# The instruction order of a hybrid attention block, made with another machine model of the scheduler

## The chip, the cores and the metric

The kernel runs on one core of one Trainium2 chip. The metric is the device time of one execution in microseconds (us). The core has five instruction streams, each worked off in its own order: PE (matmuls and transposes), DVE and POOL (elementwise work), ACT (activations and copies), and SP, which here only issues DMAs. An instruction waits for others by semaphores.

## The reference, cut to what matters

One encoder block, sequence 1024, width 1024, all in float32:

```python
h_in = rms_norm(x, norm_mix_g, 1e-6)
qa, ka, va, qb, kb, vb, ga, gb = split(h_in @ w_in)         # 512 512 512 512 512 512 1024 1024
qa, ka, qb, kb = apply_rope(...)                             # pairs of 32 in heads of 64
ya = dilated_window_attention(qa, ka, va) @ w_branch_a       # 8 heads, windows 128/512/2048 at dilation 1/4/16
o  = (softmax(q1 k1^T / 8) - lam * softmax(q2 k2^T / 8)) @ v # 4 heads: differential attention
yb = (rms_norm(o, subln_g, 1e-5) * (1 - lam_init)) @ w_branch_b
x  = x + (sigmoid(ga) * ya + sigmoid(gb) * yb) @ w_out
h2 = rms_norm(x, norm_mlp_g, 1e-6)
x  = x + square(relu(h2 @ w_ff1)) @ w_ff2                    # 1024 -> 4096 -> 1024
return rms_norm(x, norm_final_g, 1e-6)
```

## The kernel before

**Arithmetic.** Every product of float32 operands is three matmuls: each operand is split into a high part in a reduced format and a low part (`hi` by a copy on ACT, L245, and `lo` by a subtraction on POOL or DVE, L246), and hi·hi, hi·lo and lo·hi are added in PSUM. The large projections also use one level of a Strassen-like scheme with seven products for eight (`first_products`, L254; `rest_operands`, L262; `rest_products`, L274): DVE forms sums and differences of weight blocks (L265 to L268), then two groups of 24 matmuls (banks `y…` and `z…`) and one of 12 (`4…`), and DVE moves the banks out with additions (L288, L289 for `y`; L292, L294, L295 for `z`; L298 for `4`). The next group that takes the same bank has to wait for these.

**Stages.** Up to about 140 us: the first norm, the transposes and the value projections. 140 to 435 us: eight pairs of column blocks of q and k (`qk_pair`, named q8, q12, q10, q14, q0, q4, q2, q6 in this order) take turns with eight pairs of gate columns (`gate_rest`, named g4 to g7, then g0 to g3). Each finished q or k tile is rotated (`rope`, L488): four small DMAs copy the tile with its blocks of 32 rows swapped (L493, tile `rot`), DVE multiplies by the sine (L494), POOL by the cosine (L495), DVE adds (L496), ACT and DVE split into hi and lo (L504, L505), and ACT stores both. 435 to 640 us: the differential attention, four heads of eight query blocks (`b_scores`, `b_combine`, `b_values`); for each block two score banks on PE (`sb`, L689), a minimum on DVE (L692), an exponential on ACT (L694), transposes back (`tb`), a split of the result (L614 on ACT, L615 on DVE), products with v. Between them stand the remaining two products of every gate (`gate_first`, L617: banks `g1_n` and `g2_n`, 12 matmuls each, moved out by L628 on ACT). 640 to 866 us: the dilated windows; then the merge and w_out, the first MLP product to 1322, the second to 1617, and the last rows of the second MLP product with the final norm.

**What sets the order.** The source is Python that issues operations in one order. A scheduler in the framework then makes the order of each engine: it runs the program on a model of the machine, in the model's own time, and puts next on each engine the instruction that is ready there, the earlier one of the source first. So the same source gives another order when the model gives operations other durations. Semaphore waits and the turns of buffers follow from the order. The choice of the model is an argument of `tile.TileContext` (L1466), with the default in the kernel before.

## Time and profile before

| | us |
|---|---|
| three runs | 1664.23, 1668.82, 1673.82 (median 1668.82) |
| the profiled execution | 1674.86 |
| its span | 1673.1 |
| mean granted PE clock in it | 0.972 of full speed |

The profile is of one execution. A busy time is the sum over an engine's instructions, a wait is idle time of an engine in front of an instruction, put down to what released it. In rows of the timeline the first number is the start in us from the span's start, the second the length.

### The profile page before, as it was taken

The numbers are of one execution on the slowest core, as the hardware profiler recorded it, in microseconds if no ns is written. First come the engines' busy times: TensorE is split into PE (matmuls) and PEld (weight loads), VectorE is DVE, ScalarE is ACT, GpSimd is POOL, SyncE is SP. The second block draws the span as 40 slices with busy tenths as digits, with TensorE's granted clock in tenths as the row PEclk, the third lists the DMA queues.
The fourth block names the chain that finished last, engine by engine and source line by source line (L and its number), as shares of the span: only waits on it lengthen the run. The fifth ranks groups of instructions, "written<-read, shape, count | busy, mean of one in ns | idle before, by whom it ended". The sixth has DMA issues, their size and how long they took to land. (4 is left out here: it accounts for less than half of the span.)

```text
span 1673.1 us, 20932 instructions
## 1 busy us (share of the span) xinstructions
PE 1557.9 (93%) x7832; PEld 1299.2 (78%) x7832; DVE 1181.4 (71%) x1367; ACT 697.6 (42%) x1064; POOL 585.3 (35%) x289
## 2 busy tenths in 40 slices
PE   8899889988789998989999999899999989999998
PEld 6798667766577887988887878687888867888776
DVE  5976798698688996645547357644355599898984
ACT  4432122232467774544433236444444552333331
POOL 1534444555232332012220003533333344354551
PEclk8999899998999999999999999999999999999999
DMA  6367566555767557656557333444333571423112
GB/s 214 125 210 215 164 196 223 175 184 163 263 194 233 200 191 271 204 180 215 156 162 278 110 130 94 120 128 130 114 101 101 179 268 51 163 74 116 51 38 101
DMA packets 214389, 271.23 MB, mean 162 GB/s; under 512 B 12784, under 2 KB 136848, under 8 KB 214288
## 3 DMA queue, kind: packets, MB, share of 16 engines
q1 hardware_dynamic: 200464, 236.33, 44.4%
q10 hardware_dynamic: 13824, 33.56, 5.3%
q8 instruction: 62, 1.02, 0.3%
q14 instruction: 39, 0.32, 0.1%
HBM read 183.81 MB, written 80.27 MB: 158 GB/s over the span
## 5 line engine op out<-in xcount | busy, mean ns | idle before, releaser
L1359 PE MATMUL p<-b,a 128*128 128x512 f32 x392 | 154.7, 395 | 5.1 <-DVE b L1274 5.1
L1358 PE MATMUL p<-b,a 128*128 128x512 f32 x392 | 154.2, 393 | 3.0 <-ACT a L1273 3.0
L1360 PE MATMUL p<-b,a 128*128 128x512 f32 x392 | 154.4, 396 | 2.0 <-DVE a L1274 1.9
L1274 POOL TENSOR_TENSOR b<-ws,b 128x1024 fp32r<-128x1024 f32 x20 | 61.4, 3088 | 95.3 <-ACT b L1273 85.3
L1359 PEld LDWEIGHTS p<-b,a 128*128 128x128 f32 x392 | 74.2, 189 | 23.0 <-DVE b L1274 6.0
L1274 POOL TENSOR_TENSOR b<-rb,b 128x1024 fp32r<-128x1024 f32 x21 | 70.8, 3390 | 54.7 <-ACT b L1273 46.7
L1360 PEld LDWEIGHTS p<-b,a 128*128 128x128 f32 x392 | 74.0, 189 | 20.1 <-DVE a L1274 3.9
L1358 PEld LDWEIGHTS p<-b,a 128*128 128x128 f32 x392 | 74.1, 189 | 19.8 <-ACT a L1273 3.4
L689 PE MATMUL sb<-kb,qb 128*128 128x512 f32 x256 | 74.7, 416 | 15.1 <-ACT p L694 8.8
L694 ACT ACTIVATE p<-sb,mn 128x1024 f32<-128x1024 f32 x64 | 71.3, 1116 | 38.5 <-DVE mn L692 23.7
L692 DVE TENSOR_REDUCE mn<-sb 128x1 f32<-128x1024 f32 x64 | 76.8, 1217 | 9.7 <-PE sb L689 9.2
L265 DVE TENSOR_TENSOR s<-w 128x512 f32<-128x512 f32 x15 | 16.2, 1081 | 85.8 <-DMA w<-in_w_ff 85.8
L156 POOL TENSOR_SCALAR n_y<-n_ss 128x1 f32<-128x1 f32 x23 | 5.1, 222 | 187.7 <-ACT n_xn L163 183.2
L803 PE MATMUL sa<-kh_a,zq 128*128 128x256 f32 x256 | 68.9, 300 | 1.2 <-DVE mna L812 1.2
L828 DVE TENSOR_TENSOR pta<-ta,pta 128x512 fp32r<-128x512 f32 x64 | 43.8, 688 | 33.9 <-ACT pta L827 33.7
L689 PEld LDWEIGHTS sb<-kb,qb 128*128 128x128 f32 x256 | 45.9, 192 | 27.9 <-ACT p L694 13.1
L1273 ACT ACTIVATE a<-fs 128x1024 fp32r<-128x1024 f32 x28 | 29.4, 1054 | 90.6 <-PE p L1359 71.3
L803 PE MATMUL sa<-kl_a,zq 128*128 128x256 f32 x256 | 65.8, 288 | 0.0
L246 POOL TENSOR_TENSOR wt_f_l<-w,wt_f_h 128x1024 fp32r<-128x1024 f32 x15 | 36.1, 2404 | 83.0 <-ACT wt_f_h L245 70.2
L816 ACT ACTIVATE sm<-sm,mna 128x512 f32<-128x512 f32 x64 | 46.1, 720 | 32.4 <-DVE mna L812 31.8
L827 ACT ACTIVATE pta<-ta 128x512 fp32r<-128x512 f32 x64 | 37.6, 591 | 52.2 <-PE ta L823 44.5
L1145 ACT ACTIVATE c<-c 128x512 f32<-128x512 f32 x64 | 39.9, 624 | 46.6 <-DVE c L292 34.9
(442 smaller groups left out, 4966.4 us busy)
## 6 DMA issues: line engine op xcount, KB each, us to landing
w<-in_w_in SPq DMA_DIRECT2D x32, 512.0 KB, 4.3
qk<-r ACTq DMA_DIRECT2D x32, 512.0 KB, 4.8
f<-c ACTq DMA_DIRECT2D x64, 256.0 KB, 2.0
rb<-in_w_ff SPq DMA_DIRECT2D x32, 512.0 KB, 4.6
ra<-f SPq DMA_DIRECT2D x64, 256.0 KB, 5.0
w<-in_w_ff SPq DMA_DIRECT2D x30, 512.0 KB, 4.2
vb<-vb SPq DMA_DIRECT2D x16, 512.0 KB, 6.6
rot<-raw SPq DMA_DIRECT2D x64, 128.0 KB, 4.5
```

The source lines that it names most:

```text
L689: nc.tensor.matmul(sps[:, 512 * n:512 * n + 512], q[:, z, (qb % 4) * P:(qb % 4 + 1) * P], o.k[m][:, 512 * n:512 * n + 512], start=z == 0, ...
L692: nc.vector.tensor_reduce(mn, sps, axis=AX.X, op=ALU.min)
L694: nc.scalar.activation(p, sps, AF.Exp, scale=-1.0, bias=mn, accum_out=o.zz[qb][:, m:m + 1])
L803: nc.tensor.matmul(ps[:, 0:CM], zq[:, n % 4, c, :], kk[:, c * CM:(c + 1) * CM], start=c == 0 and kk is o.kh, stop=c == NCLS - 1 and kk is ...
L816: nc.scalar.activation(sm, sm, AF.Exp, scale=-1.0, bias=mn, accum_out=stat[h % 2][:, n:n + 1])
L827: nc.scalar.activation(view[0], tv, AF.Copy)
L828: nc.vector.tensor_tensor(view[1], tv, f(view[0]), op=ALU.subtract)
L1145: nc.scalar.activation(c, c, AF.Relu)
L1274: eng.tensor_tensor(lo, x, f(hi), op=ALU.subtract)
L1358: nc.tensor.matmul(acc, ah[:, i % 2, c], bh[:, i % 2, :], start=i == 0 and not more, stop=False, skip_group_check=bool(more))
L1359: nc.tensor.matmul(acc, ah[:, i % 2, c], bl[:, i % 2, :], start=False, stop=False, skip_group_check=bool(more))
L1360: nc.tensor.matmul(acc, al[:, i % 2, c], bh[:, i % 2, :], start=False, stop=last, skip_group_check=bool(more))
```

## The change

The scheduler's order is made on its timeline machine in place of its default, the core simulator. The operations of the source stay. Every engine has as many instructions as before, apart from semaphore instructions; their order is other.

```diff
-    with tile.TileContext(nc) as tc:
+    with tile.TileContext(nc, schedule_with_timeline_sim=True) as tc:
         tile_hybrid_block(tc, t, out)
```

What that moves is seen at three places. Numbers behind names are those of the program's tiles.

DVE in the projections, before, from behind the last eviction of pair q14 (`raw15`, at 266.2 us): sums of the weights of g0 and q0 (`w1_90`, `w1_80`), the evictions of gate g7 (`gc70`, `gc71`), and the rope of tile 14.

```order
L265 TENSOR_TENSOR s1_g0_2529<-w1_91_2351 128x512
L266 TENSOR_TENSOR w1_91_2351<-w1_90_2349,w1_91_2351 128x512
L289 TENSOR_TENSOR gc70_2257<-yg7_2277,gu7_2256 128x512
L267 TENSOR_TENSOR w1_80_2252<-s1_q0_2417,w1_80_2252 128x512
L267 TENSOR_TENSOR w1_90_2349<-s1_g0_2529,w1_90_2349 128x512
L268 TENSOR_TENSOR w1_80_2252<-w1_80_2252 128x512
L268 TENSOR_TENSOR w1_90_2349<-w1_90_2349 128x512
L494 SCALAR_TENSOR_TENSOR rot14_2353<-rot14_2353,sin_t_1478 128x1024
L292 TENSOR_TENSOR gc70_2257<-zg7_2278,gc70_2257 128x512
L294 TENSOR_TENSOR gc71_2258<-zg7_2278,gu7_2256 128x512
L496 SCALAR_TENSOR_TENSOR raw14_2160<-raw14_2160,rot14_2353 128x1024
L246 TENSOR_TENSOR wd_q0_l_2427<-s1_q0_2417,wd_q0_h_2426 128x512
```

After, from the same point:

```order
L494 SCALAR_TENSOR_TENSOR rot14_2353<-rot14_2353,sin_t_1478 128x1024
L494 SCALAR_TENSOR_TENSOR rot15_2367<-rot15_2367,sin_t_1478 128x1024
L496 SCALAR_TENSOR_TENSOR raw14_2160<-raw14_2160,rot14_2353 128x1024
L265 TENSOR_TENSOR s1_g0_2529<-w1_91_2351 128x512
L289 TENSOR_TENSOR gc70_2257<-yg7_2277,gu7_2256 128x512
L266 TENSOR_TENSOR w1_91_2351<-w1_90_2349,w1_91_2351 128x512
L496 SCALAR_TENSOR_TENSOR raw15_2161<-raw15_2161,rot15_2367 128x1024
L505 TENSOR_TENSOR r1_14_2362<-raw14_2160,r0_14_2361 128x1024
L267 TENSOR_TENSOR w1_90_2349<-s1_g0_2529,w1_90_2349 128x512
L267 TENSOR_TENSOR w1_80_2252<-s1_q0_2417,w1_80_2252 128x512
L292 TENSOR_TENSOR gc70_2257<-zg7_2278,gc70_2257 128x512
L294 TENSOR_TENSOR gc71_2258<-zg7_2278,gu7_2256 128x512
```

Both `rot` products, both L496 and the L505 of tile 14 now stand in front of `gc70` and `gc71` out of the `z` bank; the two L268, which end the sums of the weights of q0 and g0, come behind these (two rows further), then L295 of `gc72`, the last reader of that bank. The other pairs of the stage are changed in the same way: around q10 the two L494, both L496 and one L505 stand ahead of L292, L294 and L295 of `gc5…`.

SP behind the stores of the branch-A values (`va`), before. `vl` are copies of the values in another order for the dilated windows (L515, 18 of them), `w1_01`, `w1_11` and `w1_20` weights of the first projections of q8, g4 and q12.

```order
L515 DMA vl0_90<-va0_88 32x4x512
L251 DMA w1_01_1491<-in_w_in 128x8x128
L515 DMA vl0_90<-va0_88 32x4x512
L251 DMA w1_11_1495<-in_w_in 128x8x128
L515 DMA vl0_90<-va0_88 32x4x512
L486 DMA sin_t_1478<-in_sin_t 128x1024
L369 DMA vb1_0_94<-vb110_1404 128x4x256
L369 DMA vb1_1_95<-vb111_1405 128x4x256
L523 DMA raw8_1497<-qe0_211 128x512
L251 DMA w1_20_1589<-in_w_in 128x8x128
L369 DMA vb0_0_92<-vb010_1464 128x4x256
L369 DMA vb0_1_93<-vb011_1465 128x4x256
```

After:

```order
L515 DMA vl0_90<-va0_88 32x4x512 x3
L362 DMA va1_89<-vv101_1167 128x2x512
L515 DMA vl0_90<-va0_88 32x4x512 x3
L251 DMA w1_01_1491<-in_w_in 128x8x128
L515 DMA vl0_90<-va0_88 32x4x512 x3
L515 DMA vl1_91<-va1_89 32x4x512 x3
L251 DMA w1_11_1495<-in_w_in 128x8x128
L515 DMA vl1_91<-va1_89 32x4x512 x3
L523 DMA raw8_1497<-qe0_211 128x512
L515 DMA vl1_91<-va1_89 32x4x512 x2
L486 DMA sin_t_1478<-in_sin_t 128x1024
L515 DMA vl1_91<-va1_89 32x4x512
```

All 18 copies `vl` stand close together, most of them ahead of `w1_11`, all but one ahead of the sine table and all ahead of `w1_20` (two rows further); before, three were ahead of `sin_t` and the rest lay as far back as the middle of the projections.

ACT in the differential attention, before, where the product `g1_0` of gate 0 is moved out (L628): between the exponentials of head 2 (`p2_…`).

```order
L694 ACTIVATE p2_0_0_4476,zz2_0_4468<-sb2_0_0_4469,mn2_0_0_4474 128x1024
L694 ACTIVATE p2_0_1_4485,zz2_0_4468<-sb2_0_1_4478,mn2_0_1_4483 128x1024
L730 ACTIVATE eb1_4211<-ob1_2_4491 128x256
L614 ACTIVATE pt1_3_0_0_4517<-tb1_6_0_4521 128x4x128
L614 ACTIVATE pt1_3_1_0_4519<-tb1_6_1_4528 128x4x128
L628 ACTIVATE gp1_0_4564<-g1_0_4565 128x512
L614 ACTIVATE pt1_3_0_0_4517<-tb1_7_0_4583 128x4x128
L614 ACTIVATE pt1_3_1_0_4519<-tb1_7_1_4590 128x4x128
L694 ACTIVATE p2_1_0_4543,zz2_1_4535<-sb2_1_0_4536,mn2_1_0_4541 128x1024
L694 ACTIVATE p2_1_1_4552,zz2_1_4535<-sb2_1_1_4545,mn2_1_1_4550 128x1024
L636 ACTIVATE gq0_4560<-gq0_4560 128x512 x2
L636 ACTIVATE gq2_0_4562<-gq2_0_4562 128x512
```

After:

```order
L694 ACTIVATE p1_0_0_3904,zz1_0_3896<-sb1_0_0_3897,mn1_0_0_3902 128x1024
L730 ACTIVATE eb0_3639<-ob0_2_3919 128x256
L614 ACTIVATE pt0_3_0_0_3945<-tb0_6_0_3949 128x4x128
L614 ACTIVATE pt0_3_1_0_3947<-tb0_6_1_3956 128x4x128
L694 ACTIVATE p1_0_1_3913,zz1_0_3896<-sb1_0_1_3906,mn1_0_1_3911 128x1024
L628 ACTIVATE gp1_0_4564<-g1_0_4565 128x512
L245 ACTIVATE wa_g1_h_4849<-wgf1_4847 128x1024
L614 ACTIVATE pt0_3_0_0_3945<-tb0_7_0_4011 128x4x128
L636 ACTIVATE gq0_4560<-gq0_4560 128x512
L694 ACTIVATE p1_1_0_3971,zz1_1_3963<-sb1_1_0_3964,mn1_1_0_3969 128x1024
L614 ACTIVATE pt0_3_1_0_3947<-tb0_7_1_4018 128x4x128
L636 ACTIVATE gq0_4560<-gq0_4560 128x512
```

Gate 0 is now worked in the first blocks of head 1. On PE the 16 gate products stood between blocks of all four heads; now they stand between the first block of head 0 and the first of head 2.

In the last stage, the two halves of row block 7 (`ff_last_0`, `ff_last_1`) stand on PE between blocks 0 and 1, and block 6 is last. On DVE the end reads L1423 of block 6, L165 of block 6 (its final norm), then the two L1442 (final norm of block 7), which write a buffer that the output DMA of block 6 reads; before, L165 of block 6 stood ahead of the two L1435 of block 7 and the two L1442 at the end. In the second MLP product's first group, DVE has the evictions L1373 of the bank `p5` behind operands for later products (L1302, L1274).

## Rows read from the trace of the kernel before

**Rows 1.** The page, part 1: engine, busy us (share of span), instructions.

```profile
PE 1557.9 (93%) x7832; PEld 1299.2 (78%) x7832; DVE 1181.4 (71%) x1367; ACT 697.6 (42%) x1064; POOL 585.3 (35%) x289
```

**Rows 2.** Windows: stretch, length, PE, PEld, DVE, ACT, POOL busy, clock, DMA, GB/s.

```profile
140.00:435.00 295.00, 262.01 (x1059) 204.05 (x1059) 234.41 (x217) 71.03 (x81) 140.20 (x52) 0.95 0.62 194
435.00:480.00 45.00, 40.25 (x207) 32.61 (x208) 36.32 (x49) 30.08 (x55) 14.23 (x8) 0.96 0.78 243
480.00:539.00 59.00, 52.19 (x301) 43.77 (x300) 48.84 (x69) 40.58 (x72) 18.84 (x11) 0.97 0.63 206
539.00:592.00 53.00, 50.63 (x318) 43.89 (x317) 48.62 (x71) 40.10 (x73) 16.11 (x10) 1.00 0.67 229
592.00:640.00 48.00, 42.54 (x256) 36.10 (x255) 44.30 (x59) 33.66 (x60) 17.66 (x11) 1.00 0.56 187
```

**Rows 3.** Waits of PE, 140:435: total us, times, longest.

```profile
PE zq L237 <- DVE gc L295: 7.5, 2, 6.7
...
PE zg L237 <- DVE raw L295: 5.2, 3, 4.1
...
PE yq L237 <- DVE vc L411: 2.3, 1, 2.3
```

**Rows 4.** Timeline of DVE, from 203.71: start us, us, instruction [idle before].

```profile
203.71 1.13 DVE L265 TENSOR_TENSOR s_g<-w 128x512 f32<-128x512 f32 x1 [6.84 <-DMA w<-in_w_in]
...
214.11 0.68 DVE L295 TENSOR_TENSOR gc<-zg,gc 128x512 f32<-128x512 f32 x1
```

**Rows 5.** Timeline of PE: first matmuls of zq10, yq0, 4q0, yg0.

```profile
214.94 0.70 PE L237 MATMUL zq<-hT,wd_q_h 128*128 128x512 f32 x2
...
279.52 0.63 PE L237 MATMUL yq<-hT,ws_q_h 128*128 128x512 f32 x2
...
291.38 0.63 PE L237 MATMUL 4q<-hT,wt_q_h 128*128 128x512 f32 x2
...
294.18 0.63 PE L237 MATMUL yg<-hT,ws_g_h 128*128 128x512 f32 x2
```

**Rows 6.** DMA issues, median us to landing, and SP's timeline of five issues.

```profile
rot<-raw SPq DMA_DIRECT2D x64, 128.0 KB, 4.5
...
199.57 3.13 SPq L493 DMA_DIRECT2D rot<-raw  x5
```

**Rows 7.** Lines of DVE, 140:435: busy us, mean ns, idle before.

```profile
L496 DVE SCALAR_TENSOR_TENSOR raw<-raw,rot 128x1024 f32<-128x1024 f32 x16 | 34.1, 2132 | 2.7 <-POOL raw L495 2.3
...
L505 DVE TENSOR_TENSOR r<-raw,r 128x1024 fp32r<-128x1024 f32 x16 | 30.5, 1906 | 6.9 <-ACT r L504 4.9 <-DMA qk<-r 2.0
...
L494 DVE SCALAR_TENSOR_TENSOR rot<-rot,sin_t 128x1024 f32<-128x1024 f32 x16 | 24.1, 1509 | 2.6 <-DMA rot<-raw 2.6
```

**Rows 8.** Timeline of DVE, from 265.54.

```profile
265.54 0.69 DVE L298 TENSOR_TENSOR raw<-4q,raw 128x512 f32<-128x512 f32 x1
...
269.05 0.69 DVE L265 TENSOR_TENSOR s_g<-w 128x512 f32<-128x512 f32 x1 [2.82 <-DMA w<-in_w_in]
...
274.46 1.28 DVE L268 TENSOR_TENSOR w<-w 128x512 f32<-128x512 f32 x2
```

**Rows 9.** Window of 6.8 us: columns as in Rows 2.

```profile
401.50:408.30 6.80, 5.74 (x13) 4.05 (x14) 6.80 (x6) 2.01 (x3) 2.44 (x1) 0.50 0.73 205
```

**Rows 10.** Waits of ACT, 435:640.

```profile
ACT wa_g_h L245 <- DMA wgf<-in_w_in: 8.5, 5, 4.5
```

**Rows 11.** Waits of PE, 1330:1400.

```profile
PE p L1359 <- DVE b L1274: 5.1, 2, 5.0
```

**Rows 12.** Timeline of DVE, the last 13 us.

```profile
1660.32 1.22 DVE L1423 TENSOR_TENSOR acc<-ff_last,acc 128x1024 f32<-128x1024 f32 x1 [0.81 <-PE ff_last L1417]
...
1663.77 1.28 DVE L165 SCALAR_TENSOR_TENSOR n_xn<-acc,n_y,g_fin 128x1024 f32<-128x1024 f32 x1 [2.23 <-POOL n_y L157]
...
1668.58 1.41 DVE L1442 SCALAR_TENSOR_TENSOR n_last_xn<-acc,n_last_y,g_fin 128x512 f32<-128x512 f32 x2 [2.02 <-POOL n_last_y L157]
```

**Rows 13.** DMA issues of the output: KB each, median us to landing.

```profile
out<-n_xn SPq DMA_DIRECT2D x7, 512.0 KB, 2.6
```

## The prediction

> **What bounds the kernel now.** First read the busy times of the page: PE is busy 1557.9 of 1673.1 us, 93%, and no other engine more than 71% [rows 1]. So PE sets the time, and an order changes it only by the 115 us in which PE does nothing and by the stretches in which it runs at the lower of its two clock levels. Then read the windows by stage [rows 2]. In the projections (140 to 435 us) PE idles 33 of 295 us, and DVE is busy 234.41, so DVE has 60.6 us to spare, but it is also what PE waits for: the two longest entries of the waits in this stage are evictions L295, 7.5 us ahead of `zq` and 5.2 ahead of `zg`, and a third is an eviction too, 2.3 [rows 3]. In the differential attention the four heads take 45, 59, 53 and 48 us with DVE at 36 to 49 and PE at 40 to 52 [rows 2]: two engines that are nearly equal, with ACT between them. So I look for DVE instructions that PE waits for, and whether the new order puts something in front of them.
>
> **The change part by part.** No operation is added, so each cost is a wait.
>
> *Projections.* DVE works its list in order, so what stands ahead of an eviction delays it, even while it waits itself. Take pair q10 first. Before, DVE stands idle for 6.84 us until a weight load lets L265 go at 203.71, so since 196.9; the instruction but one before that is L298 of tile 13, which thus ends at about 196.3. From 203.71 DVE runs without a longer gap to the end of L295 (`gc52`) at 214.8, that is 11.1 us [rows 4]. zq10, which takes this bank, starts at 214.94 [rows 5]: no slack. After, both L494, both L496 and one L505 stand ahead of that L295. The rope of tile 13 needs four copies, which SP issues at 3.13/5 = 0.63 us each and which land 4.5 us after issue [rows 6]: 196.3 + 2.5 + 4.5 = 203.3. From there DVE has the same 11.1 us, less the L494 of tile 12 (1.2), which goes earlier, plus what is new in front of the L295: the L494 of tile 13 (1.2 without disturbance), its L496 (2.1) and the L505 of tile 12 (1.9), by their means [rows 7]. That is 15.1, and L295 ends at 218.4: zq10 is 3.5 us late. q14 has the same pattern and gets the same 3.5; q12, whose long wait of 6.7 us exists already, 1.
>
> Pair q0 is worse, because there the sums of its weights (L268) also stand behind the ropes. L298 of tile 15 ends at 266.2 [rows 8]; the copies land at 266.2 + 7.0 = 273.2. Before, L265 of g0 started at 269.05 and the second L268 ended at 275.7, 6.7 us [rows 8], and yq0 started at 279.52 [rows 5], 3.8 later, which is the hi copy on ACT and the lo on POOL. After, from 273.2: L494 1.2, L496 2.1, the same 6.7, and L496 2.1, L505 1.9 and two evictions of 0.68 ahead of the L268: 15.4. They end at 288.6, yq0 starts at about 292: 12 us late. For q4 and q2 the same walk, begun from a PE that is late already (so that part of the wait for the copies is covered), gives 4 and 5.5 more. The six delays are 1 + 3.5 + 3.5 + 12 + 4 + 5.5 = 29.5.
>
> Against this, ropes that are done early leave the end of the stage free: the 4.1 us stall ahead of zg2 [rows 3] should go, and with it the stretch behind it: from 401.5 on, after PE had stood idle, the granted clock is 0.50 (1.2 of 2.4 GHz) for 6.8 us [rows 9], which costs half of that, 3.4. Gain: 4.1 + 3.4 = 7.5. Sum: 29.5 - 7.5 = 22. The new stalls are as long as the old one and may bring such stretches of their own; I put none into the sum, since the rows don't tell which will, but keep them for the upper bound. Bounds: -7.5, if DVE's spare time takes up every delay and only the gain stays; 43, if nothing is recovered and four stalls bring 3.4 each.
>
> *SP at 120 to 150.* Some ten of the 18 copies `vl` are moved past `w1_11`, the weights of g4, and 12 past `raw8`. At 0.63 us an issue [rows 6] the loads behind come 6 us later. A wait of 2.3 us that PE has at yq8 [rows 3] covers part: 4 us. Bounds 0 (the weights' other users are later still) and 11 (all 18 issues).
>
> *Gates in the differential attention.* One gate product is 12 matmuls, as `4q0` is: 294.18 - 291.38 = 2.8 us [rows 5]; 16 of them are 45 us. PE's busy time over the four heads is 185.6 [rows 2], so without gates 140.8, or 35 a head. After, heads 0 and 1 hold practically all gates: 35 + 22.4 = 57.6 of PE each, while DVE needs about 48. Heads 2 and 3 have none and go at DVE's 44 to 49. With 46.5 for these: 2 x 57.6 + 2 x 46.5 = 208 against 205 now: +3. I take 5, since the first two heads can't run PE without a gap. Lower bound: the first two at DVE's 48.8 and the last two at 44.3, 186, that is -19. Upper bound: each gate's operands come late. ACT waits 8.5 us in five places for the gates' weight loads now [rows 10]; with gates twice as dense, twice that, 17, and it stands ahead of exponentials: +20.
>
> A rule of the Trainium skill speaks against this part: "Perfetto Trace Analysis", Optimization Strategy, says that where the busiest engine changes over time it may pay to interleave the regimes. The old order interleaved gates (PE) with scores (DVE) in all heads, the new one in half of them. The trace agrees so far that PE's share falls to 42.54 of 48 us in the last head, from 50.63 of 53, while DVE's stays at 92% [rows 2]. By the rule this part costs, and the sum is 40; were only the lower bound true, it would be 16.
>
> *Second MLP product, first group.* PE waits 5.1 us for DVE there already [rows 11], and evictions L1373 go behind operands that are for later: I take another such wait less what it covers, 4 (0 to 6). Elsewhere nothing on PE's path moves by more than a few us: 0, within 5 each way.
>
> *The end.* Before, block 7's two halves come last: the last L1442 starts at 1668.58 and the span ends at 1673.1, 4.5 us later [rows 12]. Block 6's eviction starts at 1660.32 as its matmuls end, and block 7 has 24 more of 2.8/12 us [rows 5], so the last matmul ends at about 1665.9 and the tail is 7.2. After, block 6 comes last. Its L165 ended at 1663.77 + 1.28 = 1665.05 [rows 12], 4.7 after its matmuls; then its output transfer, since L1442 writes the buffer that it reads, with 2.6 to landing [rows 13]; then the same 4.5. That is 11.8, 4.6 more, taken as 5. Bounds 0 and 6: the halves put between blocks 0 and 1 may fill PE's waits there.
>
> **Sum.** 22 + 4 + 5 + 4 + 5 = 40. The profiled execution took 1674.86, its span 1673.1, so 1714.9 in its terms; it is 6.0 above the median of the runs, 1668.82, so the forecast is 1709.
>
> **Rivals.**
> *The early ropes pay.* If DVE's 60.6 spare us of the stage [rows 2] take up the six delays, only the gain is left, -7.5, and if gates early let every head go at DVE's time, -19: with 13 for the rest, 1668.8 - 26.5 + 13 = 1655. For it: DVE idles in front of weight loads, 6.84 us at once [rows 4], and a rope put there costs nothing. Against it: the copies for the rope land just when that idle time ends. It decides at zq10: if that starts within 1 us of its old distance from 4q12, this holds.
> *No change.* The delays are taken up, but the heads keep their 205 us: 0 for the projections and -10 for the gates, with 13: 1672. For it: most of the moved work is on engines that aren't the bound. Against it: the bank that zq10 takes is free only 0.1 us before it starts [rows 4, 5].
> *The gates starve.* ACT stands at gate weights in the first two heads, +20 in place of 5, and the projections get 30: 1668.8 + 30 + 20 + 13 = 1732.
>
> **How the numbers follow.** The forecast's own case 0.54, gates starving 0.16, early ropes 0.17, no change 0.13. About 0.5%, 8 us, is what a measurement here can tell from no change. So faster 0.17, same 0.13, slower 0.70. The likeliest case by itself reaches from 1685 to 1730. The range takes in gates starving and nearly all of early ropes: 1653 to 1742.
>
> **What would show it.** zq10 and zq14 start 3 to 4 us later after the matmuls ahead of them than now, and yq0 about 12, with waits put down to DVE L295 and POOL `ws_q`; the stall ahead of zg2 is gone; all gate products end by the first block of head 2, heads 0 and 1 take some 58 us each, heads 2 and 3 under 48; the last matmul is followed by about 12 us. The forecast is wrong if the projections take no more than their 295 us: then DVE's order had slack that these walks didn't see.

## The result and the profile after

The changed kernel took 1680.83 us (median of six runs, 1677.32 to 1686.02), the kernel before, beside it, 1669.57 (1664.23 to 1673.82). The ratio is 1.0073, interval 1.0053 to 1.0094: about 12 us slower. The forecast had the direction, and 40 us.

The profiled execution of the changed kernel took 1677.32 us, its span is 1675.5. That is the fastest of its six, while the profiled execution of before is slower than its median: the two spans are only 2.4 us apart, so stage by stage these two traces put the changed kernel in too good a light. Part 1 of its page (engine, busy us, share, instructions) answers to [rows 1]; PE is as busy as before, so again only waits and clock can have moved the time:

```profile
PE 1557.0 (93%) x7832; PEld 1303.0 (78%) x7832; DVE 1200.7 (72%) x1367; ACT 698.1 (42%) x1064; POOL 587.0 (35%) x289
```

The windows of the changed kernel by stage, columns as in [rows 2]; its stretches are cut at its own starts of the heads:

```profile
140.00:448.00 308.00, 270.02 (x1067) 210.74 (x1067) 235.77 (x220) 71.21 (x81) 147.82 (x52) 0.93 0.56 175
448.00:513.00 65.00, 51.39 (x257) 42.20 (x257) 41.82 (x54) 37.29 (x66) 26.30 (x16) 0.92 0.73 232
513.00:563.00 50.00, 48.88 (x271) 41.39 (x271) 43.65 (x60) 38.64 (x67) 23.62 (x16) 1.00 0.79 253
563.00:612.00 49.00, 41.44 (x252) 34.24 (x252) 47.69 (x62) 34.88 (x62) 14.47 (x8) 0.97 0.67 229
612.00:660.00 48.00, 40.69 (x247) 33.57 (x245) 46.18 (x71) 31.98 (x58) 1.90 (x2) 0.96 0.54 172
```

The projections take 13 us more, at a mean clock of 0.93 in place of 0.95. Only 5 of them are idle time of PE (38.0 us in place of 33.0); 8 are busy time, of which about 2 are eight matmuls more in the stretch. Three stretches at 1.2 GHz (granted 0.50) are among the rest, one behind the start of each of yq0, yq4 and yq2, in columns as above:

```profile
286.70:293.50 6.80, 5.42 (x12) 3.73 (x13) 3.78 (x4) 1.87 (x3) 5.40 (x2) 0.50 0.69 237
327.60:334.40 6.80, 5.18 (x13) 3.60 (x12) 3.48 (x4) 1.58 (x3) 5.10 (x2) 0.50 0.69 233
368.60:375.40 6.80, 5.32 (x13) 4.16 (x14) 2.02 (x2) 1.65 (x2) 3.65 (x2) 0.50 0.75 238
```

The first head takes 65 us in place of 45, the second 50 in place of 59: the gates stand in these two now, and POOL, which makes part of their operands, is busy 26.30 and 23.62 us there and 1.90 in the last. [rows 2] does not cut the heads where they end: in before the fourth starts at 586.5, not 592, and the windows at 656.1, not 640; and the last row above ends at 660, where the windows start at 681.4. From the first scores to those of the windows the four heads take 220.8 us in before and 233.1 in the changed kernel.

PE's waits of the changed kernel in the projections (what waits, for what, total us, times, longest) answer to [rows 3]:

```profile
PE yq L237 <- DVE gc L289: 9.2, 3, 5.6
PE yq L237 <- ACT ws_q_h L245: 8.3, 3, 3.9
PE zq L237 <- DVE wd_q_l L246: 5.1, 3, 2.1
PE zg L237 <- DVE gc L295: 3.1, 1, 3.1
...
PE zq L237 <- DVE gc L295: 2.3, 1, 2.3
```

The wait of 4.1 us ahead of zg2 is gone, as foreseen, though zg3 behind it now waits 3.1. The new waits stand at the pairs' first products `yq`. The first matmul of yq0, at 279.52 in [rows 5], in the changed kernel's timeline of PE:

```profile
286.56 1.13 PE L237 MATMUL yq<-hT,ws_q_h 128*128 128x512 f32 x2 [3.92 <-ACT ws_q_h L245]
```

zq10, at 214.94 in [rows 5], has no idle time before it:

```profile
215.37 0.62 PE L237 MATMUL zq<-hT,wd_q_h 128*128 128x512 f32 x2
```

The ropes' copies, which [rows 6] have at 4.5 us from issue to landing, in the changed kernel's list of DMA issues:

```profile
rot<-raw SPq DMA_DIRECT2D x64, 128.0 KB, 2.3
```

ACT's wait for the gates' weights, 8.5 us in [rows 10], in the changed kernel's heads:

```profile
ACT wa_g_h L245 <- DMA wgf<-in_w_in: 26.0, 7, 14.6
```

PE's waits in the first group of the second MLP product, changed kernel; the 5.1 us of [rows 11] are gone:

```profile
PE p L1358 <- ACT a L1273: 3.4, 1, 3.4
PE p L1359 <- POOL b L1274: 1.0, 1, 1.0
PE p L1360 <- DVE a L1274: 0.5, 1, 0.5
```

The end, in the changed kernel's timeline of DVE, answers to [rows 12]. PE's last matmul ends at 1665.2, so the tail (from there to the span's end) is 10.3 us, where it was 7.2:

```profile
1665.21 1.23 DVE L1423 TENSOR_TENSOR acc<-ff_last,acc 128x1024 f32<-128x1024 f32 x1 [0.80 <-PE ff_last L1417]
1668.66 1.28 DVE L165 SCALAR_TENSOR_TENSOR n_xn<-acc,n_y,g_fin 128x1024 f32<-128x1024 f32 x1 [2.22 <-POOL n_y L157]
1671.02 1.42 DVE L1442 SCALAR_TENSOR_TENSOR n_last_xn<-acc,n_last_y,g_fin 128x512 f32<-128x512 f32 x2 [1.07 <-POOL n_last_y L157]
```

And a stretch of which the prediction said only that nothing moves there: from the first scores of the first window head, `sa0_0`, to those of the fourth, `sa3_0`, the kernel before takes 74.5 us, the changed one 60.1.

### The profile page after: what moved, and what is told of

It reads as the page before. It is cut to its first block, busy times and chain, and to the rows that moved or that the text cites. A ratio compares the mean times of both kernels' runs of the same rounds, so it can differ in the third digit from the quotient of the medians.

```text
span 1675.5 us, 20965 instructions
## 1 busy us (share of the span) xinstructions
PE 1557.0 (93%) x7832; PEld 1303.0 (78%) x7832; DVE 1200.7 (72%) x1367; ACT 698.1 (42%) x1064; POOL 587.0 (35%) x289
## 4 chain that ended last, share of the span: by engine, by line
PE 54%; DVE 17%; DMA 11%; issue 5%; ACT 3%; SPq 3%; POOL 2%; DVEq 0%; POOLq 0%; ACTq 0%
PE yf L237 5%; PE zf L237 5%; PE p L1360 4%; PE p L1359 4%; PE p L1358 4%; PE sa L803 3%; PE 4f L237 2%; PE yb L908 2%; PE f0f L237 2%; PE wo L1118 2%; PE wo L1116 2%; PE wo L1117 2%; PE yq L237 2%; PE f1f L237 2%; PE zq L237 2%
## 5 line engine op out<-in xcount | busy, mean ns | idle before, releaser
L1274 POOL TENSOR_TENSOR b<-ws,b 128x1024 fp32r<-128x1024 f32 x20 | 59.0, 2969 | 91.1 <-ACT b L1273 82.1
L1274 POOL TENSOR_TENSOR b<-rb,b 128x1024 fp32r<-128x1024 f32 x21 | 63.3, 3033 | 64.1 <-ACT b L1273 64.1
L1274 DVE TENSOR_TENSOR a<-fs,a 128x1024 fp32r<-128x1024 f32 x28 | 65.6, 2376 | 0.2 <-ACT a L1273 0.2
L689 PEld LDWEIGHTS sb<-kb,qb 128*128 128x128 f32 x256 | 46.3, 194 | 18.2 <-ACT p L694 10.3
L495 POOL TENSOR_TENSOR raw<-raw,cos_t 128x1024 f32<-128x1024 f32 x16 | 51.6, 3241 | 15.9 <-DMA rot<-raw 9.6
L246 POOL TENSOR_TENSOR ws_f_l<-w,ws_f_h 128x1024 fp32r<-128x1024 f32 x15 | 36.4, 2424 | 55.8 <-ACT ws_f_h L245 55.8
L237 PE MATMUL g<-hB,wa_g_h 128*128 128x512 f32 x128 | 43.4, 419 | 12.6 <-ACT gp L628 10.1
```

The source lines that it names most:

```text
L237: nc.tensor.matmul(acc, w[wz][:, k, :], hb[nm][hz][:, k, :], start=k == 0 and wz + hz == 0, stop=k == DK - 1 and wz == 1)
L246: eng.tensor_tensor(lo[:, :n, :], x, f(hi[:, :n, :]), op=ALU.subtract)
L495: nc.gpsimd.tensor_tensor(raw, raw, cos_t, op=ALU.mult)
L689: nc.tensor.matmul(sps[:, 512 * n:512 * n + 512], q[:, z, (qb % 4) * P:(qb % 4 + 1) * P], o.k[m][:, 512 * n:512 * n + 512], start=z == 0, ...
L1274: eng.tensor_tensor(lo, x, f(hi), op=ALU.subtract)
```

## The experiments

All kernels here keep the scheduler of before. One call is added, which ties each engine's instructions behind one another in the order of a table, so that the scheduler has no choice; only the table differs. The two kernels without gate loads change one line of the source besides.

```diff
     with tile.TileContext(nc) as tc:
         tile_hybrid_block(tc, t, out)
+        force_order(tc, nc)
...
+        for step in line.split():
+            at += int(step)
+            if last is not None:
+                tc.add_manual_dep(mine[at], last.name, info, reason="order")
+            last = mine[at]
```

| kernel | changed order in | median us | ratio to before, 95% interval |
|---|---|---|---|
| order_all | everything | 1676.56 | 1.0044, 1.0028 to 1.0061 |
| order_proj | all up to the first head | 1688.01 | 1.0121, 1.0104 to 1.0138 |
| order_attn | heads and windows | 1677.39 | 1.0056, 1.0035 to 1.0076 |
| order_late | behind the windows | 1668.84 | 1.0007, 0.9987 to 1.0026 |
| windows | dilated windows | 1658.19 | 0.9927, 0.9899 to 0.9955 |
| heads | differential heads | 1686.44 | 1.0079, 1.0050 to 1.0108 |
| ff2group | first group of the second MLP product | 1664.63 | 0.9957, 0.9939 to 0.9976 |
| best | windows and that group | 1652.25 | 0.9887, 0.9857 to 0.9916 |
| splits | 13 instructions in the windows | 1657.39 | 0.9925, 0.9902 to 0.9949 |
| before_noload | nothing; no gate loads | 1664.43 | 0.9966, 0.9943 to 0.9988 |
| heads_noload | heads; no gate loads | 1673.80 | 1.0030, 1.0012 to 1.0048 |
| all_acc | everything, seven loads put back | 1674.51 | 1.0038, 1.0021 to 1.0056 |
| heads_stores | heads, three stores put back | 1685.69 | 1.0090, 1.0067 to 1.0114 |
| heads_gate4 | the same, and ACT's first gate put back | 1683.17 | 1.0098, 1.0078 to 1.0118 |
| before_stores | six DMA issues at the first head | 1677.24 | 1.0056, 1.0037 to 1.0075 |
| head0 | first head | 1682.86 | 1.0082, 1.0053 to 1.0110 |
| head123 | second to fourth head | 1691.00 | 1.0123, 1.0097 to 1.0148 |

**Is it the order alone, and where?** Four kernels: the changed order through the table everywhere, and in three stretches.

> All instructions of every engine are chained to the order that the changed kernel has, and the scheduler keeps its default machine. If the order by itself makes the difference, the time is that of the changed kernel, 1.007 of before (1.005 to 1.010). If something else that came with the other machine (which of equal buffers a tile gets, semaphores) makes it, the ratio is nearer to 1.000.

> The changed order up to the end of the projections (all instructions that start before 445.7 us in the trace of the changed kernel), from there the order of before. Theory 1, each stage has its own loss or gain: the projections end 18 us later than before as in the changed kernel's trace, nothing behind them gives it back, and the ratio is 1.011 (1.008 to 1.014). Theory 2, the stage behind takes such a delay up because other engines have run ahead meanwhile: half of it or less is left, 1.000 to 1.006.

> The order of before up to the end of the projections, the changed order through differential attention and dilated windows (to 872.7 us of the changed kernel's trace), then the order of before. Theory 1: gates that are done early give back about 9 us, of these most in the dilated windows: 0.993 to 0.997. Theory 2: the gain in the changed kernel is only the projections' delay taken up, so without that delay there is none: 0.999 to 1.003. My forecast's step said +5 us: 1.003.

> The order of before up to the end of the dilated windows (868.2 us in its trace), then the changed order: merge, output projection, MLP and end. Theory 1, by the two traces: the second MLP product's first group gains 5 us, the last matmul comes another 3 earlier and the tail gets 3 longer: 0.995 to 0.999. My forecast's steps said +4 and +5 us: 1.005.

order_all works the same instructions in the same order as the changed kernel on every engine, and it is slower than before too: 1.0044, under the 1.005 that was expected at least, with an interval that just meets that of the changed kernel. So the order by itself makes a loss; whether something else adds to it is not shown.

The three stretches cover the whole order, yet 0.0121 + 0.0056 + 0.0007 = 0.0184 is four times the 0.0044 of order_all, and the ratios of order_attn and order_late lie outside all that was expected of them. So the stretches do not add up: where one order is joined to the other, waits arise that neither kernel has. One such joint is seen in the traces. PE waits ahead of `ya`, the product that opens the merge, for ACT's L888 of the last head pair, 3.4 us in before and 6.0 in the changed kernel; in order_attn and then order_late it is

```profile
PE ya L1063 <- ACT oaT L888: 10.2, 1, 10.2
...
PE ya L1063 <- ACT oaT L888: 8.4, 1, 8.4
```

From the first product `ya` to the first of the output projection, `wo`, it is 50.0 us in before, 54.1 in the changed kernel, 58.0 in order_attn and 57.2 in order_late.

The projections cost 20 us by themselves, more than the whole. So something gives time back, and the finer cut says what.

**The parts.**

> The order of before on every engine, but for the stretch of the dilated windows (656 to 864 us of before's profile), which has the changed order. Theory (in the changed order the last instructions of a head pair, which wait for a DMA or for GpSimd, stand some places further back on DVE and ACT and so block nothing): the first three window heads take 60 us in place of 71 to 75, the time falls by 11 to 14 us, less 4 to 8 if the residual loads ahead of the last head's stores on SP come with it: ratio 0.991 to 0.998. Rival (the windows' gain in the changed kernel is only operands that came earlier because the heads ahead of them were late): the windows keep their 71 to 75 us, ratio 1.000.

> The order of before, but for the stretch of the differential heads (427.8 to 681 us of before), which has the changed order. Theory (the gates' weights are asked for later against the heads' work, ACT waits for them and TensorE for ACT): sb0_0 to sa0_0 takes 235 to 240 us in place of 218 to 221, time +14 to +19 us, ratio 1.009 to 1.011. Rival (the heads are late only because the projections are late, as in the whole change): 220 us and ratio 1.000.

> The order of before, but for the first group of the second feed-forward layer (1322 to 1408 us of before), which has the changed order. Theory (the group is about 5 us shorter in the changed order, since no step of TensorE waits for the residual's rows): -5 us, ratio 0.997. The prediction on record had +4 us here: 1.002. Rival (a shorter group is given back at the group's end): 1.000.

> The order of before with the changed order in two stretches only: the dilated windows and the first group of the second feed-forward layer. If both gains stand alone and add up: -9 to -18 us, ratio 0.989 to 0.995. If the gain in the windows is lost again at their end: 0.997 or above.

Windows and first group each gain, and together they gain their sum (0.0073 + 0.0043 = 0.0116; best has 0.0113). Heads cost 13 us. Added up, projections 1.0121, heads 1.0079, windows 0.9927 and first group 0.9957 make 1.0084, and the whole change has 1.0073, but that these agree is no check: heads and windows together would make 1.0006, and order_attn, which has both, has 1.0056. By the traces 8 us of that lie behind the heads: the windows take 4.9 us longer in order_attn than in windows and the stretch from `ya` to `wo` 3.3. In order_late the same stretch takes 7 us more than in before, about as much as the first group gains.

**Why the windows gain.** ACT's timeline of before, in the third window head (start, length, instruction, idle before it): L888, the last step of the head pair before, waits 7.87 us for GpSimd and stands at the head of ACT's list meanwhile.

```profile
713.49 0.58 ACT L827 ACTIVATE pta<-ta 128x512 fp32r<-128x512 f32 x1
721.94 1.06 ACT L888 ACTIVATE oah<-sh 128x1024 fp32r<-128x1024 f32 x1 [7.87 <-POOL sh L879]
```

DVE, at the same time, stands at L889, which needs L888:

```profile
723.03 1.23 DVE L889 TENSOR_TENSOR oal<-sh,oah 128x1024 fp32r<-128x1024 f32 x1 [6.64 <-ACT oah L888]
```

Behind both stand copies `pta`, and PE waits 5.5 us for one of them (its L843 for ACT's L827). In the first window head the same is seen on a smaller scale: DVE's L760, which ends the last differential head, waits for a DMA, and PE waits 3.2 us for the `pta` of DVE's L828 behind it.

```profile
666.97 1.28 DVE L760 SCALAR_TENSOR_TENSOR eb<-eb,gsub,rrow 128x1024 f32<-128x1024 f32 x1 [3.15 <-DMA rrow<-rb]
```

The next kernel moves these steps, the chain ends, and leaves PE's and POOL's lists alone. A part of its difference on ACT:

```diff
-L888 ACTIVATE oah_6439<-sh_6393 128x1024
 L816 ACTIVATE sm_5_6435,stat_3421<-sm_5_6435,mna_5_6436 128x512
 L827 ACTIVATE pta_5725<-ta_3_6445 128x2x2x128
-L848 ACTIVATE e_6482<-ol_0_6402 128x4x4x32
 L816 ACTIVATE sm_6_6472,stat_3421<-sm_6_6472,mna_6_6473 128x512
 L827 ACTIVATE pta_5725<-ta_4_6484 128x4x128
+L888 ACTIVATE oah_6439<-sh_6393 128x1024
+L848 ACTIVATE e_6482<-ol_0_6402 128x4x4x32
```

> The order of before with 13 instructions moved in the windows and TensorE's, GpSimd's orders untouched: on DVE and ACT the chain ends of the last differential head and of the first three head pairs (eb L760, obh L763, obl L764, oah L888, oal L889) stand 3 to 7 places further back, with two copies e L848 behind their L888, one product L912 earlier and one store L766 later. Theory (in before these instructions wait for a DMA or for GpSimd at the head of an in-order engine while the window heads' own instructions are ready behind them): sa0_0 to sa3_0 takes 60 to 65 us in place of 71 to 75, the whole 7 to 14 us less, ratio 0.992 to 0.996. Rival (the windows gain by TensorE's new order or by loads that SP asks for earlier): 71 to 75 us, ratio 1.000.

13 instructions out of some 11,000 give the whole gain of the windows: 0.9925 against 0.9927. In splits L888 waits for nothing (ACT's timeline):

```profile
714.05 1.05 ACT L888 ACTIVATE oah<-sh 128x1024 fp32r<-128x1024 f32 x1
```

Part of the gain is clock. Windows of before: the first three window heads, the two stretches at 1.2 GHz (granted 0.50) in them, which begin while PE stands in these two waits, and the whole stage:

```profile
656.10:730.60 74.50, 65.78 (x463) 62.62 (x462) 41.28 (x93) 35.19 (x77) 8.65 (x4) 0.90 0.60 192
667.70:674.50 6.80, 5.58 (x26) 5.59 (x27) 5.29 (x10) 3.54 (x7) 0.00 (x0) 0.50 0.65 226
722.30:729.10 6.80, 4.87 (x23) 4.87 (x24) 3.31 (x6) 3.66 (x8) 0.00 (x0) 0.50 0.54 194
...
656.10:868.20 212.10, 197.27 (x1409) 185.11 (x1407) 118.95 (x262) 101.45 (x216) 35.06 (x15) 0.96 0.58 180
```

The same two of splits:

```profile
654.40:716.00 61.60, 60.04 (x462) 57.23 (x463) 37.94 (x88) 34.44 (x75) 9.20 (x5) 1.00 0.66 211
654.40:849.90 195.50, 190.18 (x1408) 178.76 (x1408) 119.86 (x263) 101.47 (x216) 35.51 (x16) 1.00 0.62 196
```

With as many matmuls, PE's idle time falls from 14.8 to 5.3 us, and its busy time falls by 7.1: no stretch is at 1.2 GHz any more. But before's profiled run is the longest here: nine other kernels that keep its order in this stage take 205.5 to 209.4 us. Against these the idle time falls by 5 to 9 us and the busy time by 2 to 6.

**The loads ahead of the last head pair.** In the changed order seven loads `acc` (512 KB each) stand on SP ahead of sh3 L873 and zr3 L876, on which the last window pair and then `ya` wait.

```diff
-L1078 DMA acc_8064<-in_x 128x1024
 L611 DMA st_159<-rows_z_7992 8x4x32
-L1078 DMA acc_8064<-in_x 128x1024
-L1078 DMA acc_8065<-in_x 128x1024 x4
 L145 DMA wo_r<-in_w_out 128x2x512
 L873 DMA sh_8038<-e_7920 64x1024
 L876 DMA zr_8041<-st_159 64x1024
+L1078 DMA acc_8064<-in_x 128x1024 x3
+L1078 DMA acc_8065<-in_x 128x1024 x4
```

> The changed order everywhere, but seven loads of the residual's rows (acc L1078, 512 KB each) stand on SP behind the last head pair's shift and row loads (sh3 L873, zr3 L876) and not ahead of them. Theory (the loads ahead hold up the last pair's chain, for which TensorE waits at ya0): the wait before ya0 falls from 6 to 10 us to 3.5 to 5.5, ratio to before 1.001 to 1.003, where the changed order alone has 1.0044 and 1.0073. Rival (the wait is set by DVE's and GpSimd's steps, not by the queue): 6 to 10 us stay, ratio 1.004 to 1.007.

PE's longest wait there was 6.0 us in the changed kernel and 4.0 in order_all; in all_acc it is

```profile
PE ya L1063 <- DVE ga L1072: 2.1, 1, 2.1
```

The wait fell by 2 to 4 us; the time can't tell it (1.0038 against 1.0044, intervals on each other). In the traces the stretch from `ya` to `wo` takes 50.4 us in all_acc and 54.1 in order_all, so the loads are likely to cost something there, but by the times it is not shown.

**Why the heads lose: the gates' weights.**

```diff
-        ra = col_raw(w_in, 3072 + 256 * n, f"wgf{n}", wp, "wr", 2)
+        ra = f(hb["B11"][0])[:, 0:2, :].rearrange("p k (a n) -> p (k a) n", a=4)
```

> The order of before without the eight loads of the gates' weights during the differential heads: their halves are made from a tile that is already there, so the gates' values are others. It is the partner of the same cut in the heads' changed order. Both theories: ACT's wait for these loads (8.5 us in the profile of before) goes, and since TensorE waits for no gate there, the time falls by 0 to 4 us: ratio 0.997 to 1.000.

> The changed order in the differential heads alone, without the eight loads of the gates' weights (their halves are made from a tile that is already there, so the gates' values are others). Theory (the changed order pulls the gates forward faster than their weights arrive; ACT stands 25 us at the loads and TensorE behind it): without the loads the loss goes, sb0_0 to sa0_0 about 225 us in place of 240, ratio to before 0.998 to 1.003, at most 4 us over the partner without loads in the order of before. Rival (the heads lose by TensorE's, DVE's and ACT's order among the heads' own work): 235 to 240 us, ratio 1.006 to 1.010, 12 to 16 us over the partner.

My theory fell for the most part. Without the loads the changed order still costs 1.0030 / 0.9966 = 1.0064, 11 us of 13. With the two intervals that is 6 to 15 us, so what the loads themselves cost lies between nothing and some 9 us. Where the wait went is in ACT's waits of heads_noload: the first gate's eviction now waits for another thing, the projections' last stores:

```profile
ACT gp L628 <- DMA gp<-gc: 17.5, 1, 17.5
```

**The start of the first head.** These stores stand behind the next loads on SP in the changed order, and DVE's clearing of `stat`, with which the heads begin, waits for them too. DVE's waits there, of before and then of heads:

```profile
DVE stat L918 <- DMA gp<-gc: 8.9, 1, 8.9
```

```profile
DVE stat L918 <- DMA gp<-gc: 17.7, 1, 17.7
```

heads_stores puts the three stores in front (SP, against heads); heads_gate4 moves ACT's two gate steps behind the first scores as well (ACT, against heads_stores); before_stores makes the heads' place of the stores, a gate load and two loads of k in before's order:

```diff
+L539 DMA gp_1484<-gc_3303 128x512
+L539 DMA gp_1484<-gc_3305 128x512
+L539 DMA gp_1484<-gc_3304 128x512
 L668 DMA qb_0_0_3429<-qk_80 128x1x512 x2
...
+L694 ACTIVATE p_0_0_3454,zz_0_3446<-sb_0_0_3447,mn_0_0_3452 128x1024
+L694 ACTIVATE p_0_1_3463,zz_0_3446<-sb_0_1_3456,mn_0_1_3461 128x1024
 L245 ACTIVATE wa_g_h<-wgf_3703 128x1024
 L628 ACTIVATE gp_4_3494<-g_4_3495 128x512
```

> The changed order in the differential heads alone, but on SP the three last stores of gate parts (gp3<-gc, L539) stand ahead of the first head's loads of q, in place of behind those, the next gate weight and the second head's k. Theory (stores late on SP: the wait of stat on gp<-gc is 17.7 us in the heads' changed order and 8.9 in before, and ACT's first scores come at 445.8 in place of 440.8): the wait falls to 9 to 11 us, the whole by 4 to 8 us, ratio 1.003 to 1.0055 in place of 1.0079. Rival (ACT stands at the next gate weight until 439 anyway, or the loss is made later in the heads): at most 2 us, ratio 1.0065 to 1.008.

> As heads_stores, and on ACT the first gate's copies (wa_g5_h L245 and gp L628) stand behind the first head's first two rows of scores, in place of ahead of them. Theory (the loss is the first head's start, by the stores and by ACT's wait for the weight ahead of the scores): most of the loss goes, 8 to 12 us less than the heads' changed order, ratio 0.999 to 1.003. Rival (the loss is spread over the heads): ratio 1.0055 to 1.008.

> The order of before, but on SP the three last stores of gate parts, the next gate weight's load and the second head's two loads of k stand where the heads' changed order has them: the stores last. Theory (the stores' place sets when the heads' memory comes free): the wait of stat on gp<-gc grows from 8.9 to 13 to 18 us, the first scores' step on ACT starts 2 to 5 us later, the whole 2 to 6 us more, ratio 1.001 to 1.0035. Rival (before waits there for the loads of q until 440.8 anyway, which hides it): ratio 0.999 to 1.0005.

The six issues alone cost before 9 us (1.0056), more than expected. But undoing them in the changed heads gives nothing: 1.0090 and 1.0098, with 1.0079 inside both. The first scores do start earlier on ACT, at 440.38 in heads_stores and 436.53 in heads_gate4 against 445.77; PE then waits for other things (`qb`, 5.7 us and 5.2, for which it waits 6.3 in before too, and the gates' evictions). One wait stands behind the other, and none of these was shown to be the cause by itself.

**Where in the heads.** Windows by head, first of before and then of heads:

```profile
435.30:479.60 44.30, 39.85 (x205) 32.23 (x206) 36.08 (x48) 29.68 (x54) 14.23 (x8) 0.96 0.78 240
479.60:538.60 59.00, 52.19 (x302) 43.79 (x301) 48.80 (x71) 40.58 (x71) 18.84 (x11) 0.97 0.63 207
538.60:586.50 47.90, 45.53 (x282) 39.14 (x280) 44.12 (x65) 35.97 (x65) 15.31 (x10) 1.00 0.64 216
586.50:656.10 69.60, 62.72 (x377) 53.96 (x378) 58.25 (x80) 44.29 (x78) 21.59 (x18) 0.96 0.68 233
```

```profile
432.20:500.50 68.30, 54.19 (x256) 43.26 (x257) 42.00 (x54) 37.78 (x66) 26.48 (x16) 0.88 0.73 233
500.50:550.20 49.70, 48.35 (x268) 40.91 (x267) 43.86 (x58) 38.39 (x67) 23.30 (x15) 1.00 0.79 253
550.20:601.90 51.70, 44.46 (x255) 37.44 (x254) 48.57 (x66) 35.10 (x63) 14.65 (x8) 0.90 0.64 221
601.90:672.80 70.90, 59.82 (x379) 51.12 (x377) 58.98 (x86) 40.43 (x72) 3.82 (x6) 0.95 0.48 159
```

PE's idle time by head was 4.5, 6.8, 2.4 and 6.9 us; it is 14.1, 1.4, 7.2 and 11.1, so 13.3 more, with a lower clock in the first and third. By length the first two heads take 118.0 us in place of 103.3, the last two, which have no gates left, 122.6 in place of 117.5. In five other kernels with before's order in the heads the last two take 114.9 to 120.1, and in the changed kernel itself 118.8. So nearly all of the loss is in the first head, less what the second gives back; that the last two lose for want of gates to fill DVE's pace is not shown.

> The order of before, but for the first differential head (427.8 to 479.6 us of before's profile), which has the changed order: two gates more than before stand in it. Theory A (the first head's pile of waits is what costs): 6 to 12 us more, ratio 1.004 to 1.007. Theory B (the gates pulled forward are missing later as filler): half of the loss at most here, since two gates of eight are early: ratio 1.000 to 1.003.

> The order of before, but for the second to fourth differential head (479.6 to 681 us), which have the changed order: the gates come early there and are used up before the third head ends. Theory A (the first head costs): 0 to 4 us, ratio 1.000 to 1.0025. Theory B (no filler in the last heads): 6 to 10 us more, ratio 1.0035 to 1.006.

Neither theory holds as written. Both kernels lose, and by more than half: 14 and 20 us, where the two together lose 13. In both the first head has the shape of heads: 68.6 and 70.9 us long with 14.9 and 13.7 idle (in head123 too, since its cut lets gates 6 and 7 come in ahead of the second head). So head123 does not leave the first head as it was, and the two kernels do not part the theories. In every kernel here that pulls gates into the first head, that head is longer; but in before_stores, where no gate product moves, it is 52.7 us long too, so whether it is the gates, and which of its waits would have to go, is open, and so is what head123 loses beyond that.

## Why the prediction was right in direction and wrong in size

- **Projections, +22: 20 in order_proj, but not for the reasons given.** Against the kernel windows, whose order is before's up to 656 us, the products behind the six pairs start later by steps of -1.1, 3.6, 3.4, 8.3, 5.1 and 3.3 us, sum 22.6; forecast 1, 3.5, 3.5, 12, 4 and 5.5, sum 29.5. At the first scores 17.3 are left, so 5.3 came back; forecast 7.5. (In order_proj 13.8 are left there; its other 6 come behind.) The steps were to be waits, with no new stretch at 1.2 GHz among them. But the three behind yq0, yq4 and yq2, 6.8 us each, cost up to 3.4 each by the forecast's own measure, up to 10 of the 22.6. So the waits were put too long and the clock was left to the upper bound, and that the two come out even is luck.
- **The places of these waits.** The sign was DVE's L295 ahead of zq10 and zq14. Neither waits; 9.2 us stand ahead of three `yq` for L289, an eviction of the bank `y`, which the ropes' L494 and L496 stand ahead of as well. So the mechanism, ropes ahead of an eviction, is in the trace, at another bank. For q0 the 12 was too long in two places: the copies `rot` landed after 2.3 us and not the 4.5 of [rows 6], and yq0 starts 1.2 us behind the last L268 and not 3.8. The second is PE's own new order, which the walk left out: two matmuls with the high part, then zq0's, and yq0 goes on only at 293.98, with POOL's low part long there. (By the prediction's own numbers, 288.6 + 3.8 would have been 13 late, not 12.)
- **The rival "the early ropes pay"** was to be decided at zq10, by its distance from 4q12. PE's own order moved the first matmuls of 4q12, so the product behind it, yg5, has to serve: zq10 starts 24.9 us after that, in before 19.8. That rival fell.
- **`vl` on SP, +4: not there.** yg4, right behind, starts at 157.6 where it started at 157.5.
- **Gates, +5 with -19 to +20: 13 by time,** inside the bounds, between the forecast and the rival. That all gates stand in the first two heads was right, and so was DVE's pace in the last two (busy 47.69 of 49 and 46.18 of 48 us); that the first two lose only little was not: the first has 13.6 us of idle time. The rival "gates starve" happened as told on ACT, 26.0 us in place of 8.5, and was still not the main cause: without the loads about 11 of 13 us stay. Of the rule of the Trainium skill that was weighed there ("Perfetto Trace Analysis", Optimization Strategy) the trace shows little: in the kernel heads PE's idle time in the last two heads grows by 9.1 us with the gates gone, but they take only 5.1 us longer, and 1.3 in the changed kernel.
- **Second MLP product, "another such wait less what it covers, 4 (0 to 6)": this step failed, in its sign.** ff2group gains 7 us. What PE waits for in [rows 11] is not an eviction but an operand, `b` of L1274, so evictions that move behind operands need not cost PE anything. In before that `b` takes 3.35 us on DVE and PE waits 4.96 for it; in the changed kernel and in ff2group the same `b` takes 1.22 and PE does not wait. What in the order makes it so is not shown. PE's wait in before, and the `b` that ends it:

```profile
1383.90 0.79 PE L1359 MATMUL p<-b,a 128*128 128x512 f32 x1 [4.96 <-DVE b L1274]
...
1380.49 3.35 DVE L1274 TENSOR_TENSOR b<-rb,b 128x1024 fp32r<-128x1024 f32 x1
```

- **The end, +5: nothing or less.** The tail grew by 3.1 us, from 7.2 to 10.3, but PE's last matmul comes earlier: from the first product of the second MLP it takes 324.0 us in the changed kernel and 328.3 in ff2group, which has the same first group and before's end.
- **"Elsewhere nothing on PE's path moves by more than a few us: 0, within 5 each way": this is the other step that failed.** It had no reason given. The windows gain 12 us. That a chain end goes a few places back on ACT and DVE I took for nothing. What it held up was to be read in the trace of before: L888 with 7.87 us of idle time ahead of it.

The stages of the two profiled runs, in us from one first product of PE to the next, and the least and most of other kernels that keep before's order in that stage (their number in brackets):

| stage | before | others | changed | forecast |
|---|---|---|---|---|
| start to first scores `sb` | 435.3 | 429.1 to 435.2 (5) | 448.3 | +26 |
| heads, to first `sa` | 220.8 | 217.8 to 226.2 (5) | 233.1 | +5 |
| windows, to first `ya` | 212.1 | 205.5 to 209.4 (9) | 191.3 | 0 |
| merge, to first `wo` | 50.0 | 47.6 to 51.0 (8) | 54.1 | 0 |
| output projection, to the first MLP | 93.1 | 93.1 (8) | 90.7 | 0 |
| first MLP product | 321.9 | 321.4 to 323.7 (8) | 323.7 | 0 |
| second MLP, to PE's last matmul | 332.6 | 332.4 to 337.0 (10) | 324.0 | +4 |
| tail | 7.2 | 7.2 to 7.3 (10) | 10.3 | +5 |

From the middles of the ranges the changes are +16, +11, -16, +5, -2, +1, -11 and +3, together some 7 us; the medians differ by 11, and the changed kernel's profiled run lies 3.5 under its median. So the losses that were foreseen are there, and what the forecast of 40 lacked are the 16 us of the windows and the 11 of the second MLP.

The version that keeps what gains, best, runs at 0.9887 (0.9857 to 0.9916) of before, 18.5 us under the median of before beside it.

## What to carry to other kernels

When only the order changes, look on every engine for instructions that wait long for a DMA or a slow engine while ready work stands behind them, in the old order as well as in the new: moving a handful of such chain ends back was worth more here than a new order as a whole. A longer wait on an engine is not yet a cause: take it away before you believe it, since the next wait may stand right behind it. And cut the new order into stretches: a small sum can hide losses and gains as large as itself or larger, of which one can keep the gains. But do not expect the stretches to add up, since each joint of two orders can bring a wait of its own.

## What was not expected of the hardware

- The same copies `rot` of 128 KB took 4.5 us (median) from issue to landing in before's order and 2.3 in the changed one and in order_proj (3.8 in windows, which has before's order there): nothing about the copies differs but the order around them, and which neighbour makes the difference is not shown.
- Each of the two waits of PE in before's windows, 3.2 and 5.5 us, went with 6.8 us at 1.2 GHz. Without them the stage ran at 1.00, and of the gain by the two profiles 7.1 us are busy time and 9.5 idle time (2 to 6 and 5 to 9 against other kernels with before's order).
- Six DMA issues in another order on SP cost 9 us (1.0056). With them the wait of one clearing of `stat` for the projections' last stores grew to 17.4 us from 8.9; that this wait is the whole cause is not shown, since a gate load and two loads of k moved too.
